# Six seven-product pairs in every pass over w_down, two of their four weight sums added up in DRAM ahead of time

## The chip, the core and the metric

The kernel runs on one core of a Trainium2 chip. The metric is device time in microseconds (us) of one execution; a time with its lowest and highest is the median of several executions. The profile is one further execution, recorded by the hardware profiler.

## The reference

One decoder layer: 256 tokens, model width 2048, attention in two head groups, an output projection, and a gated feed-forward layer of width 5632 with a causal convolution of width 3. All data are float32. The change lies in the feed-forward layer:

```python
h = rmsnorm(x, pre_ffn_g[l])
u = causal_dwconv(h @ w_up[l], conv_w[l], conv_b[l])       # w_up: 2048 x 11264
gate, val = jnp.split(u, 2, axis=-1)
y = (jax.nn.gelu(gate, approximate=True) * val) @ w_down[l] # w_down: 5632 x 2048
x = x + rmsnorm(y, post_ffn_g[l])
```

## The kernel before

**Products.** TensorE (PE) multiplies in a reduced form of float32, so every operand is held as a high and a low part, and a product is three matmuls: high by high, high by low, low by high. A split (`split`, L311 to L313) is a cast on ScalarE (ACT), which writes the high part `whi`, and then a subtraction on VectorE (DVE), which writes the low part `wlo`.

**The feed-forward layer in two halves.** Each half first computes 22 tiles `G` of the gated activation (128 channels by 256 tokens, high and low) in 11 groups `g`; weights of `w_up` stream in, PE fills PSUM banks, and `conv` (L892 to L906) passes each bank through ACT, DVE and GpSimd (POOL) in small ring buffers. The rings for the scaled projection (`ubuf`), for a copy (`cs`) and for gate and value (`yg`, `yv`) lie in one buffer with the tag `room`. Then come two passes over the half's rows of `w_down`, `n = 0` and `n = 2`, each for 1024 of the 2048 output columns and both token tiles. So there are four passes in all.

**A pass** (`fast_pass`, L970) walks over 11 pairs of 128-row tiles of `w_down`; pair `u` has the rows 2u and 2u+1, in an order written out by hand. A plain pair takes 2 x 2 x 2 products, 24 matmuls of 512 columns, and two weight splits of 1024 columns. A pair in `FAST` (0, 2, 4, 6) takes seven products in the manner of Strassen and Winograd, 21 matmuls. It needs four token sums, made during w_up by `token_sums` and kept in `sums`, and four weight sums, made on DVE in the pass (L1007, L1008, L1011, L1013) in the buffer `tb`. Their splits are `b11` (512 columns), `f13`, `f24` and `b2` (1024 each). Its products go to the banks m1, m5, m7, m6 ("early") and p4, p2, p3 ("late"); m6 is the fourth product and the first that reads `f24`. The last pair of a pass (the last three in the last pass) is kept back and finishes the four late banks one after the other.

**Buffers and order.** Weights come into a ring of eight: five `raw` buffers, two halves of `extra`, one third of `tb`. Splits go into a ring of five (`WB`) `whi`/`wlo` pairs. PE's order is the program's; that of ACT, DVE, POOL and of SyncE (SP), which issues the loads, is made by a scheduler while the program is built. Every engine takes its queue strictly in order, so an instruction that waits holds up all behind it. The buffer `tb` has the tag `room`, so it is the conv rings' memory and comes free when the last group's conv is done; `extra` has memory of its own, and pair 0's second tile is loaded into it early in w_up.

Of the kernel before, what the change touches and what calls it, by code (L numbers as in the profile page):

```python
# [17 lines left out]
P = 128  # L18
# [9 lines left out]
FAST = (0, 2, 4, 6)  # L28
# [3 lines left out]
def hybrid_layer(ctx: ExitStack, tc: tile.TileContext, x, pre_mix_g, w_in, b_forget, sinks,  # L32
# [33 lines left out]

    def w_load(src, a, c, pin=False):
# [4 lines left out]
        return raw, a, c  # L72

# [773 lines left out]
    with tc.tile_pool(name="ffn", bufs=1) as fp:  # L847
# [24 lines left out]
        ROOM = 4128  # L872

        def conv_room():
# [78 lines left out]
        def token_sums(into, y0, y1):  # L953

            s = fp.tile([P, 4, P], F32, tag="cst", name="s")
            a11, a21 = y0[:, 0:P], y0[:, P:256]
            a12, a22 = y1[:, 0:P], y1[:, P:256]
            dve.tensor_tensor(s[:, 0, :], a21, a22, op=ALU.add)
            dve.tensor_tensor(s[:, 2, :], a11, a21, op=ALU.subtract)
            dve.tensor_tensor(s[:, 1, :], s[:, 0, :], a11, op=ALU.subtract)  # L960
            dve.tensor_tensor(s[:, 3, :], a12, s[:, 1, :], op=ALU.subtract)
            split(into[:, 0:512], into[:, 512:UNIT], s.rearrange("p k c -> p (k c)"))
# [7 lines left out]
        def fast_pass(G, sums, order, k00, c0, load, tb, early, late, add_early, hold=1,  # L970
                      keep=None):

            left, right = slice(0, 512), slice(512, UNIT)
            fast = [u for u in order if u in FAST]
# [3 lines left out]

            def parts(src, n, into=None):
                hi, lo = into or w_parts(n)  # L980
                split(hi, lo, src)
                return hi, lo

            m1, m5, m7, m6 = early
            p2, p3, p4, p22 = late
            blocks = ((p2, 0, left), (p3, 0, right), (p4, 1, left), (p22, 1, right))
            started, held = set(), []
# [6 lines left out]
            for u in order:  # L994
                k = 2 * u
                ra, rb = (load(w_rows(w_down, k00 + k + a, 1, c0, UNIT)) for a in range(2))
                if u in FAST:
                    i = FAST.index(u)
                    end = u == fast[-1]

                    def s_of(j):
                        return (sums[:, i, j * P:(j + 1) * P],
                                sums[:, i, 512 + j * P:512 + (j + 1) * P])

                    b11 = parts(ra[:, left], 512)
                    t13, t24 = tb[:, 0, :], tb[:, 1, :]
                    dve.tensor_tensor(t13[:, left], ra[:, right], ra[:, left], op=ALU.subtract)  # L1007
                    dve.tensor_tensor(t13[:, right], rb[:, right], ra[:, right],  # L1008
                                      op=ALU.subtract)
                    f13 = parts(t13, UNIT)  # L1010
                    dve.tensor_tensor(t24[:, left], rb[:, right], t13[:, left],  # L1011
                                      op=ALU.subtract)
                    dve.tensor_tensor(t24[:, right], rb[:, left], t24[:, left],  # L1013
                                      op=ALU.subtract)
                    f24 = parts(t24, UNIT)
                    b2 = parts(rb, UNIT)
# [20 lines left out]
            if hold > 1:  # L1037
                add_early()
# [208 lines left out]
```

## Time and profile before

| | |
|---|---|
| median of 3 executions (lowest, highest) | 1064.2 us (1063.67, 1065.11) |
| the profiled execution | 1064.31 us |
| its span, first to last instruction | 1062.6 us |
| mean granted TensorE clock | 0.996 of full speed |
| first matmul of pass n=0, first half | 580.26 us |
| first matmul of pass n=0, second half | 936.94 us |

The views of the profile used below: the page (busy time by engine), the chain of work that ended last, windows (busy time in a stretch), groups of instructions by line and shape (columns: count, busy us, mean ns of one, idle before it and what ended that), the timeline (start in us, length in us, engine, line, count; in brackets the idle time before it), waits, and DMA issues (the last column is us from issue to landing).

### The profile page before, as it was taken

How to read it: one execution, taken by the hardware profiler on the slowest of the kernel's cores; microseconds unless marked ns; L12 is line 12 of the kernel's file. 1: busy time of each engine (PE TensorE's matmuls, PEld its weight loads, DVE VectorE, ACT ScalarE, POOL GpSimd, SP SyncE). 2: the span in 40 equal slices, each digit the busy share in tenths (PEclk: the TensorE clock that was granted, in tenths of full speed). 3: DMA queues.
4: the chain of work that ended last, by engine and by line, in shares of the span. 5: the costliest groups of instructions: out<-in, count | busy, mean ns of one | idle time of the engine just before them, and what ended most of it. 6: DMA issues, size and time to landing. Idle time of an engine off the chain costs nothing.

```text
span 1062.6 us, 16272 instructions
## 1 busy us (share of the span) xinstructions
PE 1049.6 (99%) x5890; PEld 914.6 (86%) x5890; DVE 839.7 (79%) x1369; ACT 639.1 (60%) x1096; POOL 229.3 (22%) x256
## 2 busy tenths in 40 slices
PE   9999999999999999999999999999999999999996
PEld 7889988888889888888888888888888888888885
DVE  5988887887467887787767999668778687789987
ACT  6767667776556765566655556446556565556551
POOL 4253335441022121211212000002121121200004
PEclk9999999999999999999999999999999999999998
DMA  8745566555773876656665666666566665656563
GB/s 280 217 120 168 162 209 202 165 170 162 282 236 107 280 231 187 193 180 185 211 188 188 193 204 206 213 196 190 169 209 188 197 197 180 194 179 200 194 242 121
DMA packets 154285, 207.08 MB, mean 195 GB/s; under 512 B 6845, under 2 KB 131037, under 8 KB 153181
## 3 DMA queue, kind: packets, MB, share of 16 engines
q1 hardware_dynamic: 153200, 203.37, 60.7%
q10 hardware_dynamic: 1004, 2.68, 0.6%
q8 instruction: 46, 0.75, 0.3%
q14 instruction: 35, 0.28, 0.1%
HBM read 201.68 MB, written 4.21 MB: 194 GB/s over the span
## 4 chain that ended last, share of the span: by engine, by line
PE 84%; DVE 9%; issue 2%; DMA 2%; ACT 2%; POOL 1%; DVEq 0%; SPq 0%; POOLq 0%; ACTq 0%
PE bank_acc L284 15%; PE bank_att L284 14%; PE bank_acc L309 12%; PE bank_att L967 9%; PE bank_acc L290 8%; PE bank_att L290 7%; PE bank_acc L253 7%; DVE wlo L313 4%; PE bank_acc L258 4%; PE bank_acc L967 2%; PE bank_att L475 1%; PE bank_att L510 1%; DVE wlo L115 1%; PE bank_acc L932 1%; DMA raw<-in_w_down_dram 1%
## 5 line engine op out<-in xcount | busy, mean ns | idle before, releaser
L115 DVE TENSOR_TENSOR wlo<-raw,whi 128x1024 fp32r<-128x1024 f32 (+3 forms) x271 | 328.5, 1224 | 127.0 <-ACT whi L112 118.4
L112 ACT CAST whi<-raw 128x1024 fp32r<-128x1024 f32 (+3 forms) x270 | 273.2, 1029 | 131.8 <-issue 88.8
L899 POOL TENSOR_TENSOR room<-room,rowf 128x256 f32<-128x256 f32 x88 | 100.3, 1160 | 393.9 <-DVE room L898 392.0
L284 PE MATMUL bank_acc<-hT,whi 128*128 128x512 f32 x736 | 173.3, 390 | 0.0
L284 PEld LDWEIGHTS bank_acc<-hT,whi 128*128 128x128 f32 x736 | 136.4, 188 | 27.4
L967 PE MATMUL bank_att<-whi,G 128*128 128x512 f32 x488 | 156.0, 389 | 0.0
L284 PE MATMUL bank_att<-hT,whi 128*128 128x512 f32 x640 | 150.6, 390 | 0.0
L284 PEld LDWEIGHTS bank_att<-hT,whi 128*128 128x128 f32 x640 | 118.7, 188 | 23.9
L967 PEld LDWEIGHTS bank_att<-whi,G 128*128 128x128 f32 x488 | 91.6, 188 | 18.9
L967 PE MATMUL bank_att<-wlo,G 128*128 128x512 f32 x244 | 95.0, 389 | 0.2 <-DVE wlo L313 0.2
L290 PEld LDWEIGHTS bank_acc<-hT,wlo 128*128 128x128 f32 x736 | 89.3, 188 | 2.0
L290 PE MATMUL bank_acc<-hT,wlo 128*128 128x256 f32 x736 | 89.8, 279 | 0.0
L901 ACT ACTIVATE room<-room,cw 128x256 f32<-128x256 f32 x88 | 53.0, 602 | 60.6 <-POOL room L899 60.6
L253 PE MATMUL bank_acc<-hT,whi 128*128 128x512 f32 x352 | 88.0, 395 | 0.0
L309 PE MATMUL bank_acc<-whi,oT 128*128 128x512 f32 (+1 forms) x272 | 81.7, 379 | 0.0
L290 PEld LDWEIGHTS bank_att<-hT,wlo 128*128 128x128 f32 x640 | 77.6, 188 | 1.7
L290 PE MATMUL bank_att<-hT,wlo 128*128 128x256 f32 x640 | 77.9, 279 | 0.0
L903 DVE SCALAR_TENSOR_TENSOR room<-room,cw 128x256 f32<-128x256 f32 x88 | 62.4, 709 | 17.6 <-ACT room L901 17.3
L253 PEld LDWEIGHTS bank_acc<-hT,whi 128*128 128x128 f32 x352 | 63.3, 188 | 11.5
L313 DVE TENSOR_TENSOR wlo<-raw,whi 128x1024 fp32r<-128x1024 f32 (+1 forms) x56 | 61.3, 1119 | 12.1 <-ACT whi L312 12.1
L312 ACT CAST whi<-tb 128x1024 fp32r<-128x1024 f32 x42 | 44.0, 1050 | 43.0 <-PE bank_att L967 19.6
L312 ACT CAST whi<-raw 128x1024 fp32r<-128x1024 f32 (+1 forms) x56 | 52.3, 958 | 27.1 <-PE bank_att L967 20.6
(254 smaller groups left out, 1594.0 us busy)
## 6 DMA issues: line engine op xcount, KB each, us to landing
raw<-in_w_up_dram SPq DMA_DIRECT2D x176, 512.0 KB, 4.2
raw<-in_w_down_dram SPq DMA_DIRECT2D x58, 512.0 KB, 4.7
raw<-in_w_in_dram SPq DMA_DIRECT2D x51, 512.0 KB, 4.7
raw<-in_w_out_dram SPq DMA_DIRECT2D x32, 512.0 KB, 4.6
extra<-in_w_down_dram SPq DMA_DIRECT2D x20, 512.0 KB, 4.7
raw<-in_w_in_dram SPq DMA_DIRECT2D x16, 384.0 KB, 3.6
tb<-in_w_down_dram SPq DMA_DIRECT2D x10, 512.0 KB, 3.5
cb<-c_dram SPq DMA_DIRECT2D x8, 256.0 KB, 3.8
```

The lines of the kernel that those rows point to most:

```text
L112: i1 = act.copy(hi[:, cs], raw[:, cs])
L115: i2 = dve.tensor_tensor(lo[:, cs], raw[:, cs], hi[:, cs].bitcast(F32), op=ALU.subtract)
L253: pe.matmul(b, parts[u][0][:, a, m * P:(m + 1) * P], hT[:, kt, :], start=(kt == 0), stop=(kt == KT - 1))
L284: pe.matmul(b, parts[u][0][:, a, m * P:(m + 1) * P], hT[:, kt, :], start=(kt == 0), stop=(kt == KT - 1))
L290: pe.matmul(b[:, 256:512], parts[u][1][:, a, m * P:(m + 1) * P], hT[:, kt, 0:256], start=False, stop=False)
L309: pe.matmul(b, a, r[:, cols], start=(first and i == 0), stop=(last and i == 2))
L312: act.copy(hi, src)
L313: dve.tensor_tensor(lo, src, hi.bitcast(F32), op=ALU.subtract)
L899: pool.tensor_tensor(u[:, 2:258], u[:, 2:258], rowf, op=ALU.mult)
L901: act.activation(y, u[:, 2:258], AF.Identity, bias=cw[:, 3, ch:ch + 1], scale=cw[:, 2, ch:ch + 1])
L903: dve.scalar_tensor_tensor(y, u[:, 1:257], cw[:, 1, ch:ch + 1], y, op0=ALU.mult, op1=ALU.add)
L967: pe.matmul(b[:, to] if to else b, a, r[:, cols], start=(first and i == 0), stop=(last and i == 2))
```

## The change

`FAST` becomes (0, 2, 4, 5, 6, 7), so each pass has six seven-product pairs and five plain ones. Another variant of the seven products is used. Two of its weight sums, together 128 x 2048 for a pair's whole width, are the same for both passes of a half and are made in DRAM: `make_sums` issues two copies on SP and two accumulating DMAs on POOL, 512 KB each, for each of 12 pairs, 48 DMAs in all. `w_load` issues one of them after every fifth load, from the 15th load on, outside the passes. In a pass a fast pair then loads three things: half of its upper tile (`b11`, 512 columns), the sums from DRAM (`r13`), and its lower tile (`r2`). DVE makes the other two sums in place, in `r2`, after `r2` has been split as `b2`; then `r2` is split again as `f24`.

The gate and value rings move to a buffer of their own, tag `gates`, which in the passes is two of the load buffers (`spare`). The buffer `room` shrinks to 2080 columns and is the sixth split buffer in the passes (`slots`). Load buffers: five `raw`, `extra`, two `spare`, and in the second half two more in the memory of `hT`. Splits made: b11, f13, b2, f24. The order of products in a pair is m1, p2, p3, m5, m7, m6, p4, in a pass's first fast pair m1, m5, m7, m6, p4, p2, p3; m6 is the first to read f24. After a pass's last fast pair the next pair is prepared ahead of the early sums, and the next pass's first pair ahead of the late blocks.

```diff
-FAST = (0, 2, 4, 6)
+EVERY, SKIP = 5, 12
+FAST = (0, 2, 4, 5, 6, 7)
...
+    def make_sums(key, k):
+        t = tc.dram_tile([P, D], F32, name="t13")
+        pair_sums[key] = t
+        to = t.rearrange("p (s x c) -> p s x c", s=2, x=2)
+        ups, downs = (w_down[(k + a) * P:(k + a + 1) * P, :]
+                      .rearrange("p (s x c) -> p s x c", s=2, x=2) for a in range(2))
+        return [lambda: sp.dma_start(to[:, :, 0, :], ups[:, :, 0, :]),
+                lambda: sp.dma_start(to[:, :, 1, :], downs[:, :, 1, :]),
+                lambda: pool.dma_start(to[:, :, 0, :], ups[:, :, 1, :], accum_op=ALU.add),
+                lambda: pool.dma_start(to[:, :, 1, :], ups[:, :, 1, :], accum_op=ALU.add)]
...
+        loads[0] += 1
+        if loads[0] % EVERY == 0 and loads[0] > SKIP and sum_steps and not paused[0]:
+            tc.keep_in_program_order(sum_steps.pop(0)())
...
-            for tag, n in (("cs", 3), ("yg", 4), ("yv", 4)):
-                rings[tag] = [room[:, at + i * 256:at + (i + 1) * 256] for i in range(n)]
-                at += n * 256
+            rings["cs"] = [room[:, at + i * 256:at + (i + 1) * 256] for i in range(3)]
+            room = fp.tile([P, 2 * UNIT], F32, tag="gates", name="room")
+            for at, tag in enumerate(("yg", "yv")):
+                rings[tag] = [room[:, at * UNIT + i * 256:at * UNIT + (i + 1) * 256]
+                              for i in range(4)]
...
+            def prepare(u):
+                k = k00 + 2 * u
+                if u not in some:
+                    return [parts(load(w_rows(w_down, k + a, 1, c0, UNIT)), UNIT)
+                            for a in range(2)]
+                b11 = parts(load(w_rows(w_down, k, 1, c0, 512)), 512)
+                r13 = load(weights[u][:, c0:c0 + UNIT].rearrange("p (a c) -> p a c", a=1))
+                r2 = load(w_rows(w_down, k + 1, 1, c0, UNIT))
+                f13, b2 = parts(r13, UNIT), parts(r2, UNIT)
+                dve.tensor_tensor(r2[:, right], r2[:, right], r13[:, left], op=ALU.add)
+                dve.tensor_tensor(r2[:, left], r2[:, left], r2[:, right], op=ALU.add)
+                return b11, b2, f13, parts(r2, UNIT)
...
-            tb = fp.tile([P, 3, UNIT], F32, tag="room", name="tb")
-            spare = [extra[:, 0, :], extra[:, 1, :], tb[:, 2, :]]
+            slots = fp.tile([P, ROOM], F32R, tag="room", name="slots")
+            slots = [slots[:, 32 + i * UNIT:32 + (i + 1) * UNIT] for i in range(2)]
+            spare = fp.tile([P, 2, UNIT], F32, tag="gates", name="spare")
+            raws, units = [fp.tile([P, UNIT], F32, tag="extra", name="extra")], [0, 0]
+            raws += [spare[:, i, :] for i in range(2)]
...
+            def parts(src, n):
+                i = units[1] % 6 - 5
+                units[1] += 1
+                hi, lo = w_parts(n) if i < 0 else [x[:, :n] for x in slots]
+                split(hi, lo, src[:, :n])
+                return hi, lo
...
-                if n == 0:
-                    order[:9] = [1, 3, 0, 5, 2, 7, 4, 8, 6]
+                      ((0, (1, 3, 0, 2, 4, 8, 5, 6, 7, 9, 10), 1),
+                       (2, (0, 2, 4, 1, 5, 6, 7, 3, 8, 9, 10), HOLD) if half else
+                       (2, (0, 2, 1, 4, 5, 3, 6, 7, 8, 9, 10), 1))]
```

Three places show how the change moves instructions. In the rows below, the number behind a name is the buffer's own; `t13_75` are the sums in DRAM of pair 2, `t13_76` those of pair 4.

SP's queue at the start of pass n=0 of the first half, before: the loads of pairs 1 and 3, then pair 0's upper tile (raw_6526; its lower tile stands 80 loads ahead of these rows, into `extra`), then pair 5.

```order
L69 DMA raw_6454<-in_w_down_dram 128x1024
L69 DMA raw_6456<-in_w_down_dram 128x1024
L69 DMA raw_6490<-in_w_down_dram 128x1024
L69 DMA raw_6492<-in_w_down_dram 128x1024
L69 DMA raw_6526<-in_w_down_dram 128x1024
L69 DMA raw_6604<-in_w_down_dram 128x1024
```

The same place now: the loads of pairs 1 and 3, pair 0's half tile, three loads each for pairs 2 and 4, and only then, into `spare`, pair 0's lower tile.

```order
L83 DMA raw_6555<-in_w_down_dram 128x1024
L83 DMA raw_6561<-in_w_down_dram 128x1024
L83 DMA raw_6591<-in_w_down_dram 128x512
L83 DMA raw_6637<-t13_75 128x1024
L83 DMA raw_6639<-in_w_down_dram 128x1024
L83 DMA raw_6674<-in_w_down_dram 128x512
L83 DMA raw_6680<-t13_76 128x1024
L83 DMA raw_6682<-in_w_down_dram 128x1024
L1138 DMA spare_6509<-in_w_down_dram 128x1024
```

What moved: pair 0's lower tile has gone from a buffer that was filled early in w_up to one that is conv's gate and value ring until the last group of w_up is done.

DVE's queue at the same time, before: the last conv output (G21), four weight sums of pair 0 in `tb`, and the low parts of its f13, f24 and b2.

```order
L313 TENSOR_TENSOR G21_3968<-room_3939,G21_3968 128x256
L1007 TENSOR_TENSOR tb_6445<-raw_6526 128x512
L1008 TENSOR_TENSOR tb_6445<-extra_6444,raw_6526 128x512
L1011 TENSOR_TENSOR tb_6445<-extra_6444,tb_6445 128x512
L1013 TENSOR_TENSOR tb_6445<-extra_6444,tb_6445 128x512
L313 TENSOR_TENSOR wlo_6536<-tb_6445,whi_6535 128x1024
L313 TENSOR_TENSOR wlo_6542<-tb_6445,whi_6541 128x1024
L313 TENSOR_TENSOR wlo_6546<-extra_6444,whi_6545 128x1024
```

Now, from two rows further on (the two rows ahead are G21 and the low part of pair 0's b2, wlo_6602; ahead of G21 stands the low part of its f13): pair 0's two sums, the low part of its f24 (wlo_6608), then the splits of pairs 2 and 4 mixed, up to the low part of pair 2's f24 in `slots`.

```order
L1019 TENSOR_TENSOR spare_6509<-spare_6509,extra_6510 128x512
L1020 TENSOR_TENSOR spare_6509<-spare_6509 128x512
L334 TENSOR_TENSOR wlo_6608<-spare_6509,whi_6607 128x1024
L334 TENSOR_TENSOR wlo_6634<-spare_6509,whi_6633 128x512
L334 TENSOR_TENSOR wlo_6642<-raw_6637,whi_6641 128x1024
L334 TENSOR_TENSOR wlo_6646<-raw_6639,whi_6645 128x1024
L334 TENSOR_TENSOR wlo_6677<-raw_6674,whi_6676 128x512
L1019 TENSOR_TENSOR raw_6639<-raw_6639,raw_6637 128x512
L334 TENSOR_TENSOR wlo_6685<-raw_6680,whi_6684 128x1024
L1020 TENSOR_TENSOR raw_6639<-raw_6639 128x512
L334 TENSOR_TENSOR wlo_6689<-raw_6682,whi_6688 128x1024
L334 TENSOR_TENSOR slots_6508<-raw_6639,slots_6508 128x1024
```

What moved: f24 of pair 0 comes from sums that can only follow the load of `spare`; and of pair 4 three splits stand ahead of pair 2's f24.

DVE's queue at the end of that pass, before: the low parts of f13, f24 and b2 of the last fast pair, 6 (wlo_6774, wlo_6780, wlo_6784), with three sums for the next pass's pair 0 among them.

```order
L313 TENSOR_TENSOR wlo_6774<-tb_6445,whi_6773 128x1024
L1007 TENSOR_TENSOR tb_6445<-extra_6444 128x512
L313 TENSOR_TENSOR wlo_6780<-tb_6445,whi_6779 128x1024
L1008 TENSOR_TENSOR tb_6445<-tb_6445,extra_6444 128x512
L1011 TENSOR_TENSOR tb_6445<-tb_6445 128x512
L313 TENSOR_TENSOR wlo_6784<-raw_6765,whi_6783 128x1024
L1013 TENSOR_TENSOR tb_6445<-tb_6445 128x512
```

Now, from the low part of pair 6's f24 (wlo_6814) to that of pair 7's f24 in `slots`: in between stand b11, f13 and b2 of pair 7, its two sums, and all four splits of the plain pairs 9 and 10 (wlo_6881, 6887, 6922, 6928).

```order
L334 TENSOR_TENSOR wlo_6814<-raw_6803,whi_6813 128x1024
L334 TENSOR_TENSOR wlo_6840<-extra_6510,whi_6839 128x512
L334 TENSOR_TENSOR wlo_6846<-spare_6509,whi_6845 128x1024
L334 TENSOR_TENSOR wlo_6850<-spare_6509,whi_6849 128x1024
L334 TENSOR_TENSOR wlo_6881<-raw_6878,whi_6880 128x1024
L1019 TENSOR_TENSOR spare_6509<-spare_6509 128x512
L334 TENSOR_TENSOR wlo_6887<-raw_6884,whi_6886 128x1024
L1020 TENSOR_TENSOR spare_6509<-spare_6509 128x512
L334 TENSOR_TENSOR wlo_6922<-raw_6919,whi_6921 128x1024
L334 TENSOR_TENSOR wlo_6928<-raw_6925,whi_6927 128x1024
L334 TENSOR_TENSOR slots_6508<-spare_6509,slots_6508 128x1024
```

What moved: the splits of the two pairs that PE needs after pair 7 now stand ahead of a split that pair 7 itself needs. In both passes of the second half the same stretch stands much the same; in pass n=2 of the first half pair 7's f24 stands right behind its sums.

More of the change, by code (lines that the diff above doesn't have):

```diff
@@ L871, in hybrid_layer @@
         ubuf, rings, cnt = [], {}, [0]
-        ROOM = 4128
+        ROOM = 2080
         def conv_room():
@@ L968, in product, with column_pass @@
                           stop=(last and i == 2))
-        def fast_pass(G, sums, order, k00, c0, load, tb, early, late, add_early, hold=1,
-                      keep=None):
+        def column_pass(G, sums, weights, some, order, k00, c0, load, parts, hold=1):
             left, right = slice(0, 512), slice(512, UNIT)
-            fast = [u for u in order if u in FAST]
+            fast = [u for u in order if u in some]
+            plain = [u for u in order[:-hold] if u not in some]
+            ready, started, held, banks = {}, set(), [], []
             def of(k, t):
                 return G[k][:, t * P:(t + 1) * P], G[k][:, 256 + t * P:256 + (t + 1) * P]
[L979 to L987, printed above, removed]
             def first(bk):
```

201 lines of the change are left out of this document (106 added, 95 removed).

## The prediction

> **What bounds the kernel now.** The page comes first: PE is busy for almost the whole span.
>
> ```profile
> span 1062.6 us, 16272 instructions
> PE 1049.6 (99%) x5890; PEld 914.6 (86%) x5890; DVE 839.7 (79%) x1369; ACT 639.1 (60%) x1096; POOL 229.3 (22%) x256
> ```
>
> The chain of work that ended last shows how fast PE goes in a pass, the windows whether it waits there (columns: PE, PEld, DVE, ACT, POOL busy, granted clock, DMA share, GB/s).
>
> ```profile
> 580.42 10.88 PE bank_att L967 x48
> ...
> 591.30 2.72 PE bank_acc L967 x12
> ```
>
> ```profile
> 580.00:637.00 57.00, 57.00 (x253) 47.18 (x252) 53.86 (x69) 30.78 (x37) 1.79 (x2) 1.00 0.61 200
> 637.00:691.00 54.00, 54.00 (x240) 44.72 (x239) 42.41 (x46) 29.92 (x31) 0.20 (x4) 1.00 0.64 207
> 940.00:997.00 57.00, 57.00 (x253) 47.19 (x252) 54.23 (x70) 33.19 (x41) 0.00 (x0) 1.00 0.57 187
> ```
>
> A matmul of 512 columns takes 10.88/48 = 0.2267 us, and in these passes PE never waits. So fewer matmuls are a gain, as long as the splits come in time. They come with little to spare: DVE is busy 53.86 of 57 us in one pass and 54.23 in another. The chain through the second half leaves PE for DVE and even for loads:
>
> ```profile
> 971.90 5.96 DMA tb<-in_w_down_dram
> ...
> 1017.18 2.88 DVE wlo L313 x3
> 1020.08 6.38 DMA raw<-in_w_down_dram
> ```
>
> **The gain.** Two more pairs in each of four passes save 3 matmuls each: 24 x 0.2267 = 5.4 us. All of it is on PE, the engine that sets the end, so without new waits the profiled execution of 1064.3 us (0.1 us from the median) would become 1058.9.
>
> **What DVE must do.** The durations, and in the timeline the distance from one start to the next:
>
> ```profile
> L313 DVE TENSOR_TENSOR wlo<-tb,whi 128x1024 fp32r<-128x1024 f32 x42 | 51.1, 1220 | 3.4 <-ACT whi L312 3.1
> L312 ACT CAST whi<-tb 128x1024 fp32r<-128x1024 f32 x42 | 44.0, 1050 | 43.0 <-PE bank_att L967 19.6 <-DVE tb L1013 16.6 <-DVE tb L1008 4.1
> ```
>
> ```profile
> 594.96 1.22 DVE L313 TENSOR_TENSOR wlo<-tb,whi 128x1024 fp32r<-128x1024 f32 x1
> 596.09 0.68 DVE L313 TENSOR_TENSOR wlo<-raw,whi 128x512 fp32r<-128x512 f32 x1
> 596.69 0.68 DVE L1011 TENSOR_TENSOR tb<-raw,tb 128x512 f32<-128x512 f32 x1
> 597.30 1.22 DVE L313 TENSOR_TENSOR wlo<-tb,whi 128x1024 fp32r<-128x1024 f32 x1
> ```
>
> In a row, 1024 columns take DVE 1.13 us (594.96 to 596.09) and 512 columns 0.61. A fast pair's three large splits, one small one and two sums are 3 x 1.13 + 3 x 0.61 = 5.2 us (before, with four sums, 6.4); PE needs only 21 x 0.2267 = 4.76 us for it. A plain pair takes DVE 2.3 us and PE 5.4. Over a pass, 6 x 5.2 + 5 x 2.3 = 42.7 us is within PE's 246 x 0.2267 = 55.8, even with 5 to 7 us for the output sums. But in a run of fast pairs DVE falls behind, and there are three in a row twice: 0, 2, 4 and 5, 6, 7, in pass n=0 of both halves and in the last pass. Before, none stood side by side. Worse, f24 is split from sums: the rows of DVE's queue have the two sums and then at once f24's low part, which must wait for ACT's cast between them: 1.05 us plus two hand-overs of about 0.1, so 1.2 us of idle DVE and 6.4 us for such a pair.
>
> **A. The start of pass n=0, twice.** Where conv ends against where PE begins the pass:
>
> ```profile
> 580.26 0.39 PE L967 MATMUL bank_att<-whi,G 128*128 128x512 f32 x1
> ...
> 585.51 0.98 DVE L313 TENSOR_TENSOR G<-room,G 128x256 fp32r<-128x256 f32 x2
> 586.52 0.69 DVE L1007 TENSOR_TENSOR tb<-raw 128x512 f32<-128x512 f32 x1
> ```
>
> ```profile
> 936.94 0.39 PE L967 MATMUL bank_att<-whi,G 128*128 128x512 f32 x1
> ...
> 942.19 0.98 DVE L313 TENSOR_TENSOR G<-room,G 128x256 fp32r<-128x256 f32 x2
> ```
>
> G21 is done 6.2 us after PE's first matmul in both halves (586.49 and 943.17). Before, that was early enough, since pair 0's tiles were loaded long ago. Now the low part of f13 stands ahead of G21 (7.4 us), and only then may SP load pair 0's lower tile into the former gate ring. How long a load takes:
>
> ```profile
> raw<-in_w_down_dram SPq DMA_DIRECT2D x58, 512.0 KB, 4.7
> ...
> tb<-in_w_down_dram SPq DMA_DIRECT2D x10, 512.0 KB, 3.5
> ```
>
> Nothing else is then in SP's queue, so I take 4.0, between the two. After it come, with 0.1 us at each hand-over, cast 1.05, low part 1.13, two dependent sums 1.4, cast 1.05: 4.9 us. f24's high part is there at 7.4 + 0.1 + 4.0 + 4.9 = 16.4 us. PE wants it after 48 matmuls of pairs 1 and 3 and 9 of pair 0, at 57 x 0.2267 = 12.9. It waits 3.5 us, and one matmul later 1.1 more for the low part (1.22 + 0.1 - 0.23). **A = 4.6 us, 9.2 for both**; with loads of 3.5 and 4.7 us, 8.2 and 10.6.
>
> [...]
>
> **B. The pair after it, twice.** DVE has no lead left. From the low part of pair 0's f24 to that of pair 2 its queue holds four rows of 512 columns and five of 1024: 2.4 + 5.7 = 8.1 us. PE does 27 matmuls in between, 6.1 us. **B = 2.0, 4.0 for both**; from 0, if PE lost as much in the same stretch for another reason, to 3.
>
> **C. The end of three passes.** Between the low parts of pair 6's and pair 7's f24 stand the four splits of pairs 9 and 10. That is 7 x 1.13 + 3 x 0.61 = 9.7 us of DVE against 21 matmuls, 4.8 us. The difference of 5.0 us is a wait, less DVE's lead at pair 6. That lead can't exceed 2.3 us: pair 6's f24 goes into the buffer of pair 5's f13, free 21 matmuls ahead (4.8 us), and cast and low part take 2.5. As pairs 5 and 6 each cost DVE 1.6 us more than PE, I take 0.6. **C = 4.4; in the middle pass, with one row less, 3.9; 12.7 in all** (8 to 15). In pass n=2 of the first half plain pairs stand between the fast ones and f24 is not overtaken: 0. For the first run of three in the last pass, where DVE starts with some lead, I take 1 (0 to 3).
>
> **What is hidden.** The 48 DMAs. PE's pace in w_up, where four loads feed 32 and 32 matmuls, then q1 and two waits:
>
> ```profile
> 565.75 7.28 PE bank_acc L284 x32
> 573.04 3.74 PE bank_acc L290 x32
> ```
>
> ```profile
> q1 hardware_dynamic: 153200, 203.37, 60.7%
> ```
>
> ```profile
> POOL room L899 <- DVE room L898: 392.0, 44, 30.9
> ...
> ACT room L901 <- POOL room L899: 60.6, 86, 3.7
> ```
>
> By q1, 0.607 x 1062.6 = 645 us of all engines for 203 MB, 512 KB cost 1.7 us. No row shows an accumulating DMA; it reads its target too, so between 1.7 and, were each stream a transfer of its own, 5 us. One of the 48 stands with every five loads, which last PE 5 x 11.0/4 = 13.8 us and cost 8.3; copies (1.7) and accumulations alternate by twos, so an accumulation may take 9.3 us before loads come late. I take 0, and 5 us in all as the upper end for the stages where loads crowd. POOL waits 392 us for DVE alone in w_up, so its issuing is hidden unless one takes several us; then ACT, which waits for `room` ahead of its casts, is late with the splits. The fast pairs' quarter megabyte more (24 x 0.26 = 6 MB) raises the passes' DMA share of about 0.6 by under a tenth. Token sums for two more groups per half lie on DVE in w_up, where it has a quarter of its time free.
>
> **The sum.** 1064.3 - 5.4 + 9.2 + 4.0 + 12.7 + 1.0 = 1085.8 us.
>
> **Rivals.**
>
> *The clock falls in A's wait.* The end and the start of this trace:
>
> ```profile
> 1052.00:1055.00 3.00, 0.07 (x1) 0.00 (x0) 1.70 (x6) 1.08 (x5) 2.24 (x2) 1.00 0.52 198
> 1055.00:1062.00 7.00, 0.00 (x0) 0.00 (x0) 3.32 (x5) 0.00 (x0) 1.24 (x2) 0.51 0.43 150
> ```
>
> ```profile
> 6.40 2.05 PE L221 MATMUL bank_att<-hT,whi 128*128 128x512 f32 x4
> 8.25 1.05 PE L226 MATMUL bank_att<-hT,wlo 128*128 128x256 f32 x4
> ```
>
> 3 us after the last matmul the granted clock is 0.5. At the start, four matmuls took 1.85 us, 0.46 each, until about 9 us after PE began. A's wait of 3.5 us is as long. Nine us at half speed cost 4.5, twice; part of it would have been B's wait, so 5 to 9 more: 1091 to 1095. [...] 13%. [...]
>
> *DVE keeps its lead: faster.* If the loads of `spare` come in time and the low parts are there in runs of three, all that is left is the 5.4 us: 1058.9. It decides at a lead of 5 us at pair 7's f24. For it: PE waits nowhere in the passes of before. Against it: five split buffers and a sixth allow no more than 2.3 us, and the load can't start sooner. 4%; with half of the waits, 1070, 5%.
>
> *The DRAM sums are dear.* If an accumulating DMA holds the 16 engines for over 9.3 us, loads are late from the attention on, each of the 24 by the excess: 1 us over gives 1110. For it: nothing here bounds its price from above. Against it: it would have to cost more than five copies. 10%.
>
> *It doesn't do what it says:* the sums land too late for the pass. In POOL's queue all four steps of pairs 0 and 2 stand in the attention, long ahead. Under 1%.
>
> **How the numbers follow.** Forecast 68%, from 1075 (A 8.2, B 0, C 8, the last run 0) to 1094 (10.6, 6, 15, 3), or 1099 with 5 for the DMAs; clock 13%, half the waits 5%, dear sums 10%, full lead 4%. The range 1074 to 1099 leaves out the full lead, the half and the dear sums, 19%. A measurement of this kernel can tell about 0.2% (2 us) from no change; of the case of half the waits a fifth might end there. Faster 4%, same 1%, slower 95%.
>
> **What would show it.** Right: PE idle 3 us or more just behind 57 matmuls of each n=0 pass, ended by ACT's cast from `spare`; a second pair of waits some 7 us later; 4 us before pair 7's sixth product in three passes; 24 matmuls fewer at 0.2267. Wrong: PE busy through the passes as before, or new waits ahead of 580 us.

## The result, and the profile after

| | before | after |
|---|---|---|
| median of 4 executions each, same chip (lowest, highest) | 1064.65 us (1063.67, 1065.84) | 1099.03 us (1096.70, 1100.12) |
| ratio after to before, 95% interval | | 1.0319 (1.0299 to 1.0340) |
| the profiled execution | 1064.31 us | 1100.12 us |
| its span | 1062.6 us | 1098.4 us |
| mean granted TensorE clock | 0.996 | 0.983 |

The change makes the kernel 34.4 us slower; the forecast was 1085.8 us with a range up to 1099. The page of the kernel after, busy time by engine and the granted clock in 40 slices of the span:

```profile
span 1098.4 us, 16433 instructions
...
PE 1062.6 (97%) x5866; PEld 916.9 (83%) x5866; DVE 855.5 (78%) x1389; ACT 648.6 (59%) x1116; POOL 249.4 (23%) x280
...
PEclk9999999999999999999998989999999999989988
```

PE has 24 matmuls less than before, 5866 for 5890, as planned, and yet 13 us more of busy time: matmuls have become longer somewhere. The clock row says where: in the slices of the passes it is not full. In the page of the kernel before, it was full up to the last slice, in which the matmuls end:

```profile
PEclk9999999999999999999999999999999999999998
```

**Where PE waits.** The timeline of the kernel after at the start of the first pass n=0 (start, length, engine, line, count; in brackets the idle time before it and what ended it; rows left out are marked with dots):

```profile
588.68 0.42 DVE L334 TENSOR_TENSOR G<-room,G 128x256 fp32r<-128x256 f32 x1
...
589.13 0.80 SPq L1138 DMA_DIRECT2D spare<-in_w_down_dram  x2
...
593.73 0.84 PE L992 MATMUL bank_acc<-slots,sums 128*128 128x512 f32 x3
594.03 1.05 ACT L333 CAST whi<-spare 128x1024 fp32r<-128x1024 f32 x1 [6.22 <-DMA spare<-in_w_down_dram]
...
598.97 0.79 PE L992 MATMUL bank_acc<-whi,sums 128*128 128x512 f32 x1 [4.40 <-ACT whi L333]
600.23 0.80 PE L992 MATMUL bank_acc<-wlo,sums 128*128 128x512 f32 x1 [0.47 <-DVE wlo L334]
...
601.68 0.63 PE L992 MATMUL bank_att<-wlo,G 128*128 128x512 f32 x1
602.11 1.06 PE L992 MATMUL bank_att<-whi,G 128*128 128x512 f32 x2
```

This is wait A with its whole chain: G21 is done (588.68 + 0.42 = 589.10), SP issues the load into the former gate ring (589.13), ACT starts the first cast 4.9 us later (594.03), and the cast of f24, made from the sums, lets PE go on at 598.97. A wait is read here as the distance from one start to the next less the 0.23 us of a matmul: 598.97 - 594.18 (the last of the three) - 0.23 = 4.56, and 1.03 for the low part. The last two rows show what nobody waits for: from 601.68 to 602.11 one matmul took 0.43 us instead of 0.23.

The end of the same pass, DVE's rows from the low part of pair 6's f24 to that of pair 7's, and PE's waits:

```profile
628.48 1.23 DVE L334 TENSOR_TENSOR wlo<-raw,whi 128x1024 fp32r<-128x1024 f32 x1 [1.19 <-ACT whi L333]
...
635.97 2.35 DVE L334 TENSOR_TENSOR wlo<-raw,whi 128x1024 fp32r<-128x1024 f32 x2
...
637.18 0.50 PE L992 MATMUL bank_acc<-slots,sums 128*128 128x512 f32 x1 [1.72 <-ACT slots L333]
638.24 1.22 DVE L334 TENSOR_TENSOR slots<-spare,slots 128x1024 fp32r<-128x1024 f32 x1
...
639.51 1.22 PE L992 MATMUL bank_acc<-slots,sums 128*128 128x512 f32 x2 [1.83 <-DVE slots L334]
```

From low part to low part DVE takes 638.24 - 628.48 = 9.76 us, the 9.7 of the forecast, and PE waits twice about 2 us: wait C. Counted over the 21 matmuls from pair 6's f24 to pair 7's, PE is 4.5 us late.

**Where the clock falls.** Windows of the kernel after, each 3.41 us long, as is the stretch at 0.50 from 1010.33 on (us; busy time of PE, PEld, DVE, ACT, POOL with counts; granted clock; DMA share; GB/s):

```profile
593.91:597.32 3.41, 0.66 (x3) 0.20 (x2) 2.14 (x3) 1.05 (x1) 0.00 (x0) 1.00 0.01 4
597.32:600.73 3.41, 1.29 (x2) 0.79 (x3) 2.24 (x4) 2.85 (x4) 0.00 (x0) 0.50 0.52 154
600.73:604.15 3.42, 3.42 (x9) 2.68 (x9) 3.05 (x5) 1.22 (x2) 0.00 (x0) 0.50 0.69 226
...
607.56:610.97 3.41, 1.98 (x7) 1.07 (x7) 3.38 (x5) 1.05 (x1) 0.00 (x0) 1.00 0.36 141
634.87:638.28 3.41, 1.10 (x4) 0.34 (x2) 3.41 (x5) 1.92 (x3) 0.00 (x0) 1.00 0.93 286
638.28:641.69 3.41, 2.18 (x5) 1.79 (x6) 2.67 (x5) 0.00 (x0) 0.00 (x0) 0.50 1.00 373
641.69:645.11 3.42, 3.42 (x9) 2.65 (x9) 2.92 (x4) 1.04 (x1) 0.00 (x0) 0.50 0.69 253
965.96:969.37 3.41, 0.22 (x2) 0.01 (x1) 2.18 (x4) 1.10 (x2) 0.00 (x0) 1.00 0.17 55
969.37:972.78 3.41, 2.95 (x6) 2.05 (x7) 3.41 (x4) 2.36 (x3) 0.00 (x0) 0.50 0.42 109
972.78:976.20 3.42, 3.42 (x9) 2.64 (x9) 1.96 (x3) 1.10 (x2) 0.00 (x0) 0.50 0.77 254
1006.92:1010.33 3.41, 1.01 (x3) 0.65 (x4) 3.41 (x4) 1.04 (x1) 0.00 (x0) 1.00 0.97 323
1010.33:1013.75 3.42, 3.42 (x9) 2.65 (x9) 3.10 (x5) 1.04 (x1) 0.00 (x0) 0.50 0.86 282
1058.12:1061.53 3.41, 1.18 (x4) 0.38 (x3) 3.41 (x4) 2.38 (x3) 0.00 (x0) 1.00 1.01 428
1061.53:1064.94 3.41, 2.10 (x5) 1.71 (x6) 3.31 (x5) 0.00 (x0) 0.00 (x0) 0.50 0.98 413
1064.94:1068.36 3.42, 3.42 (x9) 2.65 (x9) 2.29 (x3) 1.04 (x1) 1.83 (x1) 0.50 0.05 19
```

The clock is 0.50 in whole stretches: it falls at 597.32, 638.28, 969.37 and 1061.53 for two windows each and at 1010.33 for one, that is behind both waits A and behind all three waits C. In each case the window ahead of the fall held 0.2 to 1.2 us of matmuls. A window with 1.98 us (wait B, 607.56) has no fall behind it. A full window at half clock counts 9 matmuls; at full clock, 3.41 / 0.2267 = 15 fit.

### The profile page after: what moved, and what is told of

Read it like the earlier page. It is cut to its first block, busy times and chain, and to the rows that moved or that the text cites. A ratio compares the mean times of both kernels' runs of the same rounds, so it can differ in the third digit from the quotient of the medians.

```text
span 1098.4 us, 16433 instructions
## 1 busy us (share of the span) xinstructions
PE 1062.6 (97%) x5866; PEld 916.9 (83%) x5866; DVE 855.5 (78%) x1389; ACT 648.6 (59%) x1116; POOL 249.4 (23%) x280
## 4 chain that ended last, share of the span: by engine, by line
PE 76%; DVE 11%; DMA 4%; issue 4%; ACT 4%; POOL 1%; DVEq 0%; SPq 0%; POOLq 0%; ACTq 0%
PE bank_acc L305 15%; PE bank_att L305 13%; PE bank_acc L330 9%; PE bank_acc L311 8%; PE bank_att L311 7%; PE bank_acc L274 7%; PE bank_att L992 7%; DVE wlo L334 4%; PE bank_acc L279 4%; PE bank_acc L992 2%; DVE slots L334 2%; ACT whi L333 1%; DMA spare<-in_w_down_dram 1%; DMA raw<-in_w_out_dram 1%; PE bank_att L496 1%
## 5 line engine op out<-in xcount | busy, mean ns | idle before, releaser
L136 DVE TENSOR_TENSOR wlo<-raw,whi 128x1024 fp32r<-128x1024 f32 (+3 forms) x271 | 332.8, 1241 | 110.5 <-ACT whi L133 102.8
L992 PE MATMUL bank_att<-whi,G 128*128 128x512 f32 x342 | 117.6, 404 | 0.0
L333 ACT CAST whi<-raw 128x1024 fp32r<-128x1024 f32 (+1 forms) x69 | 65.1, 973 | 46.2 <-DVE raw L1020 24.1
L334 DVE TENSOR_TENSOR wlo<-raw,whi 128x1024 fp32r<-128x1024 f32 (+1 forms) x69 | 76.7, 1139 | 19.7 <-ACT whi L333 19.7
L992 PEld LDWEIGHTS bank_att<-whi,G 128*128 128x128 f32 x342 | 67.6, 198 | 14.8
L992 PE MATMUL bank_att<-wlo,G 128*128 128x512 f32 x171 | 69.5, 407 | 0.6 <-DVE wlo L334 0.6
L330 PEld LDWEIGHTS bank_acc<-whi,oT 128*128 128x128 f32 x272 | 50.2, 188 | 9.3
```

The source lines that it names most:

```text
L136: i2 = dve.tensor_tensor(lo[:, cs], raw[:, cs], hi[:, cs].bitcast(F32), op=ALU.subtract)
L330: pe.matmul(b, a, r[:, cols], start=(first and i == 0), stop=(last and i == 2))
L333: act.copy(hi, src)
L334: dve.tensor_tensor(lo, src, hi.bitcast(F32), op=ALU.subtract)
L992: pe.matmul(b[:, to] if to else b, a, r[:, cols], start=(first and i == 0), stop=(last and i == 2))
```

## Experiments

All times are medians, beside executions of the kernel before on the same chip (1064.2 to 1064.5 us in these). Waits are summed over the four passes as above; "half-speed matmuls" are those at a distance of about 0.43 us. The kernel after had 31.3 us of waits and 49 half-speed matmuls in its profile, each of which costs 0.2 us. The numbers behind a wait in the lists of waits are us in total, times, and the longest.

### e1_fill: matmuls of zeros in the waits

```diff
+                if fill and i < 2:
+                    for _ in range(fill[0][i]):
+                        pe.matmul(fill[1], zeros, G_now[0], start=False, stop=False)
                 pe.matmul(b[:, to] if to else b, a, r[:, cols], start=(first and i == 0),
```

> The kernel after, with matmuls of zeros (same shape and pace as the others, added to an open bank) put in front of the matmuls that wait: 18 or 13 and then 3 at pair 0 of each pass n=0, 7 and then 6 at pair 7 of three passes. They run inside waits that are there anyway. Theory (the half clock comes from PE being idle in these waits): in the kernel after, 49 matmuls ran at a distance of about 0.43 instead of 0.227 us, 10 us in all; with the waits filled no stretch at half clock is left, and the time is 1088 (1086 to 1091). Rival (the clock falls for another reason, for instance the load on the DMAs): the same five stretches at the same places, 1098 to 1100.

Measured: 1088.80 us (1087.74 to 1089.71), ratio 1.0227 (1.0211 to 1.0243), mean clock 0.998. The timeline of e1_fill where A was:

```profile
594.75 4.35 PE L995 MATMUL bank_att<-G,zeros 128*128 128x512 f32 x18
599.02 0.50 PE L996 MATMUL bank_acc<-whi,sums 128*128 128x512 f32 x1
...
601.08 0.40 PE L996 MATMUL bank_att<-wlo,G 128*128 128x512 f32 x1
601.31 0.62 PE L996 MATMUL bank_att<-whi,G 128*128 128x512 f32 x2
```

The product with f24 starts at 599.02, about as late as before; what it waits for has not changed. But the zeros run in the gap, and behind it matmuls go at 0.23 us. No half-speed matmul is left, and the time falls by 1099.0 - 1088.8 = 10.2 us. So the half clock was worth 10 us, and it came from PE standing idle; the loads and DMAs are those of the kernel after, and without the idle time they make no fall.

### e2_tile_early: pair 0's lower tile in a buffer that is free early

```diff
+                turned = u == fast[0] and u != order[0]
+                if not turned:
+                    b11 = parts(load(w_rows(w_down, k, 1, c0, 512)), 512)
...
                 f13, b2 = parts(r13, UNIT), parts(r2, UNIT)
+                if turned:
+                    r11 = load(w_rows(w_down, k, 1, c0, 512))
...
                 if u == fast[0]:
-                    steps = steps[0:1] + steps[3:] + steps[1:3]
+                    steps = (steps[0:1] + steps[3:] + steps[1:3] if u == order[0] else
+                             steps[3:5] + steps[1:3] + steps[5:] + steps[0:1])
```

> The kernel after, but in pass n=0 pair 0's lower tile and its sums go into buffers that are free early; its half tile goes into the former gate ring, and the product that needs it comes last in the pair. Theory of the prediction (wait A is the load that can only start after conv's last operation): A goes (5.6 and 4.4 us in the profile of after), B shrinks to about 1 us in each half because DVE starts its queue earlier, and the two stretches at half clock behind A go (about 5 us): 1080 (1078 to 1084). Rival (A is the backlog of ACT and DVE at conv's end, the load is only what shows): PE still waits over 3 us for pair 0's f24, 1092 or more.

Measured: 1086.50 us (1086.27 to 1087.96), ratio 1.0211 (1.0197 to 1.0225). A is gone, and so are its two stretches at half clock: the 29 half-speed matmuls left all stand behind C. But the time is 2.5 us above the expected range. The timeline of e2_tile_early, PE's waits at the start of the first pass n=0:

```profile
596.90 0.50 PE L992 MATMUL bank_att<-wlo,G 128*128 128x512 f32 x1 [0.83 <-DVE wlo L334]
...
601.23 0.73 PE L992 MATMUL bank_acc<-slots,sums 128*128 128x512 f32 x2 [1.29 <-DVE slots L334]
```

Both are in pair 2, for its b2 and its f24. A and B together had cost 7.6 us in the first half and 6.0 in the second; 2.7 and 3.3 us of waits have stayed in their place, where I had expected 1. So the load was the cause of A. (The edit also moves the product with f24 from the fourth to the fifth place of pair 0, but that is 3 matmuls, 0.7 us, of 5.6.) The pairs behind it have no lead of their own, and a part of what they wait for is still a load into the former gate ring: DVE's row of the low part of pair 2's b11, whose half tile is loaded into `spare` together with pair 0's.

```profile
593.53 0.69 DVE L334 TENSOR_TENSOR wlo<-spare,whi 128x512 fp32r<-128x512 f32 x1 [1.21 <-ACT whi L333]
```

DVE stands 1.21 us idle there, ahead of the splits for b2 and f24. How the 2.7 us divide between that and DVE's own work was not tested.

### e3_splits_behind: pair 7's f24 no longer overtaken

```diff
-                            nxt = order[i + 1]
-                            ready[nxt] = prepare(nxt)
+                            for nxt in order[i + 1:]:
+                                ready[nxt] = prepare(nxt)
...
-                split(hi, lo, src[:, :n])
+                i1 = act.copy(hi, src[:, :n])
+                i2 = dve.tensor_tensor(lo, src[:, :n], hi.bitcast(F32), op=ALU.subtract)
+                if pin:
+                    tc.keep_in_program_order(i1)
+                    tc.keep_in_program_order(i2)
```

(`pin` is true for the plain pairs behind the last fast one.)

> The kernel after, with the splits of the plain pairs behind the last fast pair kept behind everything that the program has ahead of them, so that pair 7's f24 is not overtaken by four splits; nothing else. Theory of the prediction (C is the overtaking): C falls from 4.5 to about 1 us in each of three passes and takes its stretches at half clock with it (3 of 5, about 5 us): 1099 - 10 - 5 = 1084 (1081 to 1087). Rival (DVE has no lead in a run of three fast pairs, and whatever is put later waits later): C falls to about 1.5 us, but the same 9 us turn up as waits of the next fast pairs, behind the splits that are now late; the waits add up to what they were within 2 us, and the time is 1092 to 1099.

Measured: 1095.19 us (1093.09 to 1095.78), ratio 1.0286 (1.0272 to 1.0300): the rival. The timeline of e3_splits_behind, DVE at the end of the first pass n=0, then PE in the pass that follows:

```profile
633.38 1.23 DVE L1147 TENSOR_TENSOR slots<-spare,slots 128x1024 fp32r<-128x1024 f32 x1 [1.17 <-ACT slots L1146]
634.52 4.62 DVE L1147 TENSOR_TENSOR wlo<-raw,whi 128x1024 fp32r<-128x1024 f32 x4
...
657.55 0.69 PE L992 MATMUL bank_acc<-slots,sums 128*128 128x512 f32 x1 [2.08 <-ACT slots L1146]
659.63 1.22 PE L992 MATMUL bank_acc<-slots,sums 128*128 128x512 f32 x2 [1.40 <-DVE slots L1147]
```

The four plain splits (634.52, 4.6 us) now follow f24, and C, counted over the same 21 matmuls, falls from 12.9 to 5.4 us over the three passes. But DVE stands 1.17 us idle ahead of f24, waiting for the cast, and whatever is put behind is late in its turn: at 657.55 and 659.63, in the next pass, PE waits 4.1 us that were not there, and the second half has its own of this kind. The waits still add up to 29.2 us, 2.1 less than in the kernel after, and 33 matmuls instead of 49 run at half speed, which is 3.2 us. Together they are the 5.1 us between the profiled spans (1098.4 and 1093.3); the medians differ by 3.8.

### e4_dmas_alone: the kernel before with the 48 DMAs

```diff
+        loads[0] += 1
+        if loads[0] % EVERY == 0 and loads[0] > SKIP and sum_steps and not paused[0]:
+            tc.keep_in_program_order(sum_steps.pop(0)())
```

> The kernel before, with the 48 DMAs (24 copies on SP, 24 accumulating DMAs on POOL, after every fifth load) and nothing else of the change; what they make in DRAM is not used. Theory of the prediction (they are hidden behind PE): 1064.6, within 0.7 us of before, and no wait of PE in w_up. Rival (the 1.1 us that the kernel after is late between 310 and 350 us is theirs): 1065.5 to 1066. Dear sums: 1070 or more.

Measured: 1064.25 us (1063.09 to 1066.68) against 1064.46, ratio 1.0003 (0.9995 to 1.0012): no difference, though the interval alone would leave room for 1.3 us. The page of e4_dmas_alone, the queues (packets, MB, share of 16 engines) and the DMA issues (the last number is us to landing):

```profile
q0 software_dynamic: 6528, 12.58, 8.3%
...
t<-in_w_down_dram SPq DMA_DIRECT2D x24, 512.0 KB, 6.9
t<-in_w_down_dram POOLq DMA_DIRECT2D x24, 512.0 KB, 8.4
```

Queue q0 holds the accumulating DMAs alone: 0.083 x 1063.4 / 24 = 3.7 us of all engines for one, between the bounds of 1.7 and 5 and far below the 9.3 us at which, by the forecast's estimate, loads would be late. The 1.1 us that the profile of after was late between 310 and 350 us are no steady cost of the DMAs either: the profiles of e2_tile_early and e3_splits_behind, which issue the same DMAs there, lose less than 0.1 us in that stretch against before, and in e4_dmas_alone PE is busy for all 50.00 us from 300 to 350, with 316 matmuls as in before.

### e5_f24_ready: the other two sums in DRAM too, for pairs 2, 4 and 7

```diff
+FOUR = (2, 4, 7)
...
+        return [lambda: sp.dma_start(to[:, :, 1, :], downs[:, :, 1, :]),
+                lambda: sp.dma_start(to[:, :, 0, :], downs[:, :, 0, :]),
+                lambda: pool.dma_start(to[:, :, 1, :], t13[:, :, 0, :], accum_op=ALU.add),
+                lambda: pool.dma_start(to[:, :, 0, :], to[:, :, 1, :], accum_op=ALU.add)]
...
+                if u in FOUR:
+                    b2, f13 = parts(r2, UNIT), parts(r13, UNIT)
+                    r24 = load(lows[u][:, c0:c0 + UNIT].rearrange("p (a c) -> p a c", a=1))
+                    return b11, b2, f13, parts(r24, UNIT)
```

> The kernel after with its orders and buffers, but the other two weight sums of pairs 2, 4 and 7 are made in DRAM too (24 more DMAs; from w_up on one after every third load), so these pairs load f24 ready: DVE makes no sums for them, and their f24 waits for no other split. DVE's work for such a pair is 3 x 1.13 + 0.61 = 4.0 us against PE's 4.76. Theory (B, C and the wait of the last pass come from DVE's work per pair being above PE's pace in runs of three): these waits go, 3.6 + 13.1 + 1.6 = 18 us in the profile of after, and with C its three stretches at half clock, 29 slow matmuls x 0.2 = 6 us; A stays with its two: 1099 - 18 - 6 = 1075 (1072 to 1078). Rival (the passes are then short of loads, 12 x 512 KB more, or 72 DMAs are no longer hidden): new waits ended by a DMA, 1082 or more.

Measured: 1071.58 us (1071.06 to 1072.41), ratio 1.0068 (1.0054 to 1.0082). PE's waits in the passes of e5_f24_ready (for what; us in total, times, longest):

```profile
PE bank_acc L1007 <- ACT whi L348: 6.6, 2, 3.4
PE bank_acc L1007 <- DVE wlo L349: 1.1, 2, 0.6
```

What is left are the two waits A and their low parts, nothing else. B, C and the wait of the last pass are gone, with the stretches at half clock behind C (the 22 half-speed matmuls left all stand behind A). The gain is 27 us where I had expected 24: beside the 18 us of those waits some small ones went.

### e6_both: e5 and e2 together

> The kernel e5_f24_ready together with the change of e2_tile_early at pair 0. Theory (A is pair 0's load; B, C and the rest are DVE's work per pair; the half clock is the waits): no wait of PE over 0.5 us in the four passes, no stretch at half clock before the last matmul, and the 24 matmuls fewer show: 1064.5 - 5.4 = 1059 (1058 to 1061, where the upper end has 2 us for 72 DMAs). Rival (one of them is only shifted, as in e3_splits_behind): waits of 5 us or more in all, 1065 or more.

Measured: 1059.73 us (1058.55 to 1061.22) against 1064.38, ratio 0.9955 (0.9942 to 0.9967). This kernel is faster than the kernel after and, by 0.4%, than the kernel before. Of e6_both, the page (busy time), PE's waits in the passes and the granted clock:

```profile
PE 1042.9 (99%) x5866; PEld 907.9 (86%) x5866; DVE 836.2 (79%) x1365; ACT 648.0 (61%) x1116; POOL 259.2 (24%) x292
```

```profile
PE bank_att L1007 <- DVE wlo L349: 0.2, 1, 0.2
```

```profile
core 0: 1058.0 us, clock 0.997
```

With the waits gone the clock stays up (0.997 on the mean), and the 24 matmuls show: 4.7 us of the 5.4. By the medians that leaves 0.7 us for the 72 DMAs and all else; by the interval it could be up to 1.9.

### e7_no_three: no three fast pairs side by side

```diff
-                      ((0, (1, 3, 0, 2, 4, 8, 5, 6, 7, 9, 10), 1),
-                       (2, (0, 2, 4, 1, 5, 6, 7, 3, 8, 9, 10), HOLD) if half else
-                       (2, (0, 2, 1, 4, 5, 3, 6, 7, 8, 9, 10), 1))]
+                      ((0, (1, 3, 0, 2, 8, 4, 5, 9, 6, 7, 10), 1),
+                       (2, (0, 2, 1, 4, 5, 3, 6, 7, 8, 9, 10), HOLD) if half else
+                       (2, (0, 1, 3, 2, 4, 8, 5, 6, 9, 7, 10), 1))]
```

(against e2_tile_early)

> The kernel e2_tile_early with orders of pairs in which no three fast pairs stand side by side (n=0: 1 3 0 2 8 4 5 9 6 7 10; n=2: 0 1 3 2 4 8 5 6 9 7 10, last pass 0 2 1 4 5 3 6 7 8 9 10). Nothing is taken from DVE. The prediction's reason for C (three in a row and four splits of plain pairs ahead of f24): C and the wait of the last pass go, 14.6 us, and three stretches at half clock, 6 us: 1086.5 - 21 = 1066 (1064 to 1070). Rival (it is DVE's work for a whole stretch of pairs and sums at the seam of two passes, whatever the order): the waits move to the pairs around the seams and add up to 10 us or more, 1076 to 1087.

Measured: 1087.09 us (1084.94 to 1088.29), ratio 1.0211 (1.0197 to 1.0225), as e2_tile_early: the rival. The timeline of e7_no_three, PE's waits at the seam of the two passes of the second half:

```profile
1011.00 0.50 PE L992 MATMUL bank_acc<-whi,sums 128*128 128x512 f32 x1 [1.84 <-DVE y_sb L1129]
...
1012.78 0.50 PE L992 MATMUL bank_acc<-wlo,sums 128*128 128x512 f32 x1 [1.27 <-DVE wlo L334]
...
1017.45 0.50 PE L992 MATMUL bank_att<-wlo,G 128*128 128x512 f32 x1 [0.97 <-DVE wlo L334]
...
1022.32 0.50 PE L992 MATMUL bank_acc<-slots,sums 128*128 128x512 f32 x1 [2.08 <-ACT slots L333]
...
1023.79 0.73 PE L992 MATMUL bank_acc<-slots,sums 128*128 128x512 f32 x2 [0.98 <-DVE slots L334]
```

The waits have left the ends of the runs. Half of them, 11.5 us in the two halves, stand where the output sums and the next pass's first fast pairs meet. All add up to 22.8 us against 23.8 in e2_tile_early. So "three in a row" is not needed for the waits; it is the place where they showed. One caution: more than the runs of three changed, since an order also sets which pair stands at the seam.

### e8_fill_part: fewer zeros, and at C alone

The edit is that of e1_fill with (3, 3) at C and none at A.

> The kernel after, with zero matmuls only at C, three and three instead of seven and six, and none at A. At C the two waits of about 2 us then have 0.7 us of work each. Theory (the clock falls when a stretch of some 3.4 us between fixed points in time is mostly idle): in the profile of after such a stretch ahead of each fall at C held about 1.1 us of matmuls; with 0.7 to 1.4 us more it is over half busy, so the three falls at C go and the two at A stay: 1099 - 6 = 1093 (1091 to 1095). Rival (two idle times of over 1 us close together are enough): all five stay, 1098 to 1100.

Measured: 1093.86 us (1091.89 to 1094.93), ratio 1.0272 (1.0257 to 1.0288). Two of the three falls at C are gone, the two at A are there, and one at C is left, for one window instead of two. Windows of e8_fill_part ahead of the fall that stayed and around a wait of C without one:

```profile
634.89:638.30 3.41, 1.26 (x5) 0.74 (x5) 3.41 (x4) 0.97 (x1) 0.00 (x0) 1.00 1.00 364
1003.50:1006.90 3.40, 2.35 (x10) 1.62 (x9) 3.40 (x5) 2.25 (x3) 0.00 (x0) 1.00 0.81 247
```

Behind the window with 2.35 us of matmuls nothing fell, behind that with 1.26 the clock did; the granted clock is 0.989 on the mean, for 0.983 in the kernel after. The rival is out, since the two idle times close together are there in all three places; but "over half busy" was not reached everywhere.

### e9_sums_unused: the sums made, but not waited for

The edit is against e5_f24_ready.

```diff
                 if u in FOUR:
                     b2, f13 = parts(r2, UNIT), parts(r13, UNIT)
+                    dve.tensor_tensor(r2[:, right], r2[:, right], r13[:, left], op=ALU.add)
+                    dve.tensor_tensor(r2[:, left], r2[:, left], r2[:, right], op=ALU.add)
                     r24 = load(lows[u][:, c0:c0 + UNIT].rearrange("p (a c) -> p a c", a=1))
```

> The kernel e5_f24_ready, but DVE makes the two sums of pairs 2, 4 and 7 all the same, in place in their lower tiles, and nothing uses them: DVE has the work back (2 x 0.61 = 1.2 us for each of these pairs, 14.6 us in 12), but f24 no longer waits for it. Theory 1 (B and C are the chain low part of b2, two sums, cast, low part, in which DVE stands idle at the cast or has other splits ahead of f24's): the waits stay away but for a little, 1071.6 + 0 to 4 = 1072 to 1076. Theory 2 (they are DVE's work, 5.2 us a pair against PE's 4.76): most of the 14.6 us comes back at the ends of the runs of three, with half clocks: 1082 or more.

Measured: 1076.66 us (1075.28 to 1077.99), ratio 1.0120 (1.0103 to 1.0137), just above the range of theory 1 and far from theory 2. (This run was on another chip than e5_f24_ready; the ratios to before, 1.0120 and 1.0068, give the same distance.) PE's waits in the passes of e9_sums_unused:

```profile
PE bank_acc L1007 <- ACT whi L348: 6.6, 2, 3.4
PE bank_acc L1007 <- DVE wlo L349: 2.5, 4, 0.8
```

DVE has all of its work back, 14.6 us, and only 5.1 us of time come back with it (3.5 in the profiled spans, 1073.6 for 1070.1). So of the 27 us that e5_f24_ready gained about a fifth was DVE's work, and the rest, with the half clock behind it, the chain through the sums: f24 could start only after b2 and both sums, stood behind other splits, and left DVE idle at its cast. How much each link of this chain is worth was not taken apart.

## Why the prediction came out as it did

**The waits were right, in place and in size.** The forecast against what the profile of after shows (us):

| step | predicted | profile of after |
|---|---|---|
| A, both halves | 9.2 | 10.0 (5.6 and 4.4) |
| B, both halves | 4.0 | 3.6 (2.0 and 1.7) |
| C, three passes | 12.7 | 12.9 (4.5, 4.0, 4.4) |
| first run of three in the last pass | 1.0 | 1.6 |
| sum | 26.9 | 28.1 |
| 24 matmuls fewer | -5.4 | -5.4 (24 x 0.2267; e6_both shows 4.7) |
| DMAs | 0 | 0 (e4_dmas_alone) |

A's load took 4.9 us from issue to cast where 4.0 was taken, and its chain followed row by row. That the load was A's cause is shown by e2_tile_early, where A vanished with it.

**The term that was mis-sized is the clock.** The forecast set it to nothing, and gave 13% to a rival in which it falls at A and costs 5 to 9 us. It fell at A twice and at C three times, and e1_fill prices all five falls at 10.2 us: without them the kernel would have been at 1088.8, 3 us from the forecast. The step that failed is the reading of the end of the trace, "A's wait of 3.5 us is as long": I took an unbroken idle time of 3 us as the condition, so C's two waits of 2 us were never looked at. The rival's price was off too: it took nine us at half speed from the start of the trace, but a fall lasted 3.4 or 6.8 us and cost about 2. That 1099.0 still lies at the very edge of the range is luck: the edge was worked out from longer waits and 5 us for the DMAs, which cost nothing, and not from the clock.

The windows show another condition: how much PE did in a stretch of 3.41 us, and there two waits with one matmul between them did the same as one (1.10, 1.01 and 1.18 us busy ahead of the falls at C, 0.66 and 0.22 at A). The length of an idle time in one piece does not decide. PE's waits in the kernel after ahead of the fall at 1010.33, then those of e7_no_three at the seam, with the matmuls behind them:

```profile
1008.03 0.50 PE L992 MATMUL bank_acc<-slots,sums 128*128 128x512 f32 x1 [1.77 <-ACT slots L333]
1009.83 0.81 PE L992 MATMUL bank_acc<-slots,sums 128*128 128x512 f32 x2 [1.29 <-DVE slots L334]
```

```profile
1011.00 0.50 PE L992 MATMUL bank_acc<-whi,sums 128*128 128x512 f32 x1 [1.84 <-DVE y_sb L1129]
1012.78 0.50 PE L992 MATMUL bank_acc<-wlo,sums 128*128 128x512 f32 x1 [1.27 <-DVE wlo L334]
1013.12 0.40 PE L992 MATMUL bank_acc<-whi,sums 128*128 128x512 f32 x1
1013.35 0.39 PE L992 MATMUL bank_att<-whi,G 128*128 128x512 f32 x1
1013.58 0.40 PE L992 MATMUL bank_att<-wlo,G 128*128 128x512 f32 x1
```

Behind 1.77 and 1.29 us the clock fell; behind 1.84 and 1.27 us the matmuls go on at a distance of 0.23 us. Nor does the busy time of the profile decide so close to the border, as two windows of e7_no_three show:

```profile
365.74:369.15 3.41, 1.56 (x11) 1.47 (x12) 2.83 (x6) 3.41 (x6) 0.00 (x0) 1.00 1.01 362
645.63:649.04 3.41, 1.71 (x6) 1.22 (x7) 3.14 (x5) 3.41 (x4) 0.00 (x0) 1.00 0.29 106
```

Behind the first, with 1.56 us of matmuls, no fall follows; behind the second, with 1.71, the clock falls. What decides there stays open.

The falls of the kernel after lie at fixed distances: the other four are 40.96, 372.05, 413.01 and 464.21 us behind the first, which is 12, 109, 121 and 136 times 3.413 us (40.96 / 12); the shortest fall was as long, from 1010.33 to 1013.74. Four of the five falls lasted two windows: in the first of the two PE was still waiting for a part (busy for 1.29, 2.18, 2.95 and 2.10 us of 3.41). The fall at 1010.33 had a full window behind it and lasted one.

**C's size was right, its reason only in part.** I put it down to the four plain splits ahead of f24 and to a run of three. e3_splits_behind took away the first and e7_no_three, on top of e2_tile_early, the second, and in both the waits went elsewhere and added up to almost as much. What e5_f24_ready and e9_sums_unused show in its place is the dependence itself: as long as f24 must follow b2, two sums and a cast within one pair's time, and DVE has no lead, some split is late. The remark "6.4 us for such a pair", with DVE idle at the cast, was nearer to it than the counting of overtaking splits. B goes with the dependence too (e5_f24_ready); with A alone gone, about 3 us of waits stay in each half (e2_tile_early).

**The rivals.** "DVE keeps its lead" (1058.9) is what e6_both does, once f24 is ready in DRAM and pair 0's tile is loaded early. "Dear sums" is out by e4_dmas_alone. For the whole, the profiled executions close the sum: -5.4, 31.3 us of waits with the small ones, and 49 x 0.2 = 9.8 for the half clock are 35.7 of the 35.8 us between the two spans. The early 1.1 us is made up by an end that is 1.0 us shorter.

## What to carry to other kernels

When a kernel runs PE without a gap, saved matmuls are worth something only if the operands still come ahead of time: count the chain of each operand (load, cast, sums, cast again) against PE's time for one unit of work, and where it is tight, take the dependence away rather than shuffle the queue. Where a wait can't be avoided, price the clock with it: here it fell behind stretches of 3.41 us with 0.2 to 1.2 us of matmuls, and five falls cost 10.2 us. Matmuls of zeros in the gaps held it at 0.998 here, and the product they stood ahead of started at 599.02 us instead of 598.97 in the first pass n=0 (e1_fill). Sums of weights that are needed more than once can be made in DRAM by DMAs; here 48 of them changed the time from 1064.46 to 1064.25 us (e4_dmas_alone).

## What the runs showed of the hardware

- **The granted clock fell behind stretches with little work of PE.** In the profile of after it fell to 0.50 five times between matmuls, at distances that are multiples of 3.413 us, each time behind a window of 3.41 us with 0.22 to 1.18 us of matmuls. It fell behind windows with 1.26 us (e8_fill_part) and 1.71 us (e7_no_three) as well, and did not behind windows with 1.56 us (e7_no_three), 1.98 us (after, 607.56) and 2.35 us (e8_fill_part). It came back behind windows in which PE was busy for all of the 3.41 us, and not behind those with 1.29, 2.10, 2.18 and 2.95 us (after). A fall lasted 3.4 or 6.8 us and cost some 2 us (10.2 us for five).
- **Matmuls of zeros into an open bank** held the clock at 0.998 of full speed on the mean, for 0.983 without them: 76 of them in all (18, 3, 7 and 6 in the first pass n=0) were worth 10 us (e1_fill).
- **An accumulating DMA from DRAM to DRAM** of 512 KB took 3.7 us of the 16 engines and 8.4 us to landing, a plain copy 6.9 us to landing (e4_dmas_alone). 48 DMAs of both kinds cost no time that could be measured (-0.5 to 1.3 us by the interval), and 72 left 0.7 us for all that e6_both lost (up to 1.9).
